# Block kernel on one core: the opening stage, its modulation products and its first norm, written anew

## The chip, the cores and the metric

The kernel runs on one core of one Trainium2 chip. The metric is the device time of one execution in microseconds (us); lower is better. In the tables of the profile PE is TensorE, PEld its weight loads, DVE is VectorE, ACT is ScalarE, POOL is GpSimd, and SP is SyncE, whose queue issues nearly all loads.

## The reference, cut to what matters

Two layers of a hybrid block are computed in fp32 for 256 tokens of x and 256 tokens of ctx, with a model width of 1024. Each layer first makes modulation vectors out of c and c_ctx, and then a half feed-forward block, a mixing block, and a second half feed-forward block. What the opening stage needs of it:

```python
mod_x = silu(c) @ ada_w + ada_b            # [9 * 1024]
mod_c = silu(c_ctx) @ ada_w + ada_b
sx, sc = split(mod_x, 9), split(mod_c, 9)  # shift, scale, gate, ...
h = x * rsqrt(mean(x * x) + EPS) * ffn1_norm
y = h * (1 + scale) + shift                # scale: chunk 1, shift: chunk 0
a, g = split(y @ wi, 2)                    # wi: 1024 x 5632
x = x + 0.5 * gate * ((silu(g) * a) @ wo)
```

The same is done for ctx with its own vectors. The first feed-forward block of layer 0 can begin only when shift (chunk 0) and scale (chunk 1) are there.

## The kernel before, in words

Features lie on partitions: x and ctx together are eight tiles of 128 features x 512 tokens (256 of x, 256 of ctx). A large product is made of three fp32r products of high and low parts (`mm3`, L181: lines 183, 184 and 185), so each weight tile is first split into a high part by ACT (L171) and a low part by DVE (L172).

The modulation weights come in slabs of 512 output columns and 1024 rows, 2 MB each, so that chunk 0 (shift) is slabs 0 and 1, and chunk 1 (scale) is slabs 2 and 3. `run` loads, in the order of the string `START = "02f1f3"`, slab 0, slab 2, the first up-weight tile (`f`, 1 MB), slab 1, the second up-weight tile and slab 3, behind the constants, the vectors and x. `ada_pe` makes the product of a slab: four rows (the high and the low part of c and of c_ctx) times the weights, one product for each of eight k tiles in plain fp32 (L301, for the first two k of slabs 0 and 1), or, for the others, two fp32r products (L298, L299) behind a split of the weight tile by ACT and DVE; then a copy of the row out of PSUM (L303), four small products that put the row on partitions (L306), and the bias (L308). `STARTC = "xr0s2d13D"` is the order in which this is written: sums of squares (x), the norm's factor (r), slab 0, the factor on all partitions (s: `spread`, L231 and L233), slab 2, the scale for features 0 to 511 (d: `derive`, L366), slabs 1 and 3, the scale for the other half (D).

`norm` (L427, L430, L431) multiplies x with scale and factor on DVE, adds the shift on ACT (which gives the high part yh), and makes the low part yl on DVE, tile by tile of 128 features x 256 tokens, the first four of the eight feature tiles first. `ffn` then runs the up-projections: 22 steps f, each 48 products of 128x512 (8 k tiles, value and gate, three products each), then SiLU (L550), the product with the value (L551) and the split of the result. In the first block the first two steps are woven: both take k 0 to 3, then both take k 4 to 7. Between the steps `fill` places pieces of other work (further modulation vectors on DVE, hyena filters).

A scheduler orders each engine's instructions by the order of the text and by when it reckons their inputs to be there; each engine then works strictly in that order. A product of plain fp32 is two instructions on PE, an fp32r product is one.

Of the kernel before, what the change touches and what calls it, by code (L numbers as in the profile page):

```python
# [9 lines left out]
F32 = mybir.dt.float32  # L10
# [29 lines left out]
LATE = (0, 0, 0, 0)  # L40
F1 = (1.9, 0, 1)
F2 = (0.8, 0, 1.0, 20)
WARM = 30
PIECES = 2
ADA = (6, 6, 8, 8)
START = "02f1f3"
STARTC = "xr0s2d13D"
# [13 lines left out]
class Builder:  # L61
    def __init__(self, ctx, tc, t, out):
        self.tc, self.nc, self.t, self.out = tc, tc.nc, t, out
        self.uid = 0
        self.ready = []
# [73 lines left out]
    def consts(self):  # L139
        nc, t = self.nc, self.t  # L140
        self.ident = self.const([P, P], name="ident")
        nc.sync.dma_start(out=self.ident, in_=t["k_ident"])
# [63 lines left out]
    def rsqrt_cols(self, ps, n):  # L206
        """ps [P, n, 2]: v and -v/2. One after the other column by column, so that the columns' chains overlap."""
# [17 lines left out]
    def bcast(self, r, ntile):  # L225
        """r [tokens, ntile] per token -> PSUM [128, ntile*128], the same on every partition."""
# [24 lines left out]
    def ada_init(self):  # L251
        nc, t = self.nc, self.t
        craw = self.const([P, KT, 2], name="craw")
        nc.sync.dma_start(out=craw, in_=t["cvec"])
        nc.scalar.activation(self.cvec, craw, AF.Silu)
        self.c4 = self.const([P, KT, 4], F32R, name="c4")
        for v in range(2):
            self.split(self.c4[:, :, 2 * v], self.c4[:, :, 2 * v + 1], self.cvec[:, :, v])
        self.c40 = self.const([P, KT, 4], name="c40")
        nc.gpsimd.memset(self.c40, 0.0)  # L260
        for v in range(2):
            nc.gpsimd.tensor_copy(self.c40[:, :, 2 * v], self.cvec[:, :, v])
        self.sum4 = self.const([4, 2], name="sum4")
        nc.gpsimd.dma_start(out=self.sum4, in_=t["k_sum4"])
# [9 lines left out]
    def ada_fetch(self, l, slab, pools):  # L274
        """The weights of a slab, by k."""
# [12 lines left out]
    def ada_pe(self, l, slab, ws, split):  # L288
# [3 lines left out]
        ps = self.pa((4, 512))  # L292
        for k, w in enumerate(ws):
            first, last = k == 0, k == KT - 1
# [7 lines left out]
        row = self.tmp((4, 512), name="row")  # L302
        nc.scalar.copy(row, ps)  # L303
# [7 lines left out]
    def ada_group(self, l, chunks, vecs):  # L311
        """Yields after each piece of work."""
# [72 lines left out]
    def sumsq(self, m, lo, n):  # L385
        """Adds the squares of tokens lo..lo+n of feature tile m."""
# [11 lines left out]
    def rstd(self, lo, n):  # L398
        """Each token's 1/rms, tokens on partitions."""
# [11 lines left out]
    def spread(self, lo, r):  # L411
        """The same on every partition."""
# [4 lines left out]
    def norm(self, l, name, T):  # L417
        nc = self.nc
        yh = [self.yp.tile([P, T], F32R, tag="y", name=self.nm("yh")) for _ in range(KT)]
        yl = [self.yp.tile([P, T], F32R, tag="y", name=self.nm("yl")) for _ in range(KT)]  # L420
        parts = 2 if self.ready else 1
        kp = KT // parts
        for v, ks in [(v, range(p * kp, p * kp + kp)) for p in range(parts) for v in range(T // S)]:
            s = slice(v * S, v * S + S)
            for k in ks:
                a = self.nyp.tile([P, S], F32, tag="ny", name=self.nm("ny"))
                nc.vector.scalar_tensor_tensor(a, self.x[k][:, s], self.gs[l, name, v][:, k:k + 1], self.rb[v],  # L427
                                               op0=ALU.mult, op1=ALU.mult)
                sh = self.shift(l, name, v)[:, k:k + 1]
                nc.scalar.activation(yh[k][:, s], a, AF.Identity, bias=sh)  # L430
                nc.vector.scalar_tensor_tensor(yl[k][:, s], a, sh, yh[k][:, s].bitcast(F32), op0=ALU.add, op1=ALU.subtract)  # L431
# [64 lines left out]
    def ffn(self, l, name, T, fill, last=1):  # L496
        nc = self.nc
        wi, wo = self.t[name + "_wi"][l], self.t[name + "_wo"][l]
        first = bool(self.ready)
        early = T == S and not first  # L500
        if early:
            zh, zl = self.scaled(l, name)
        yh, yl = self.norm(l, name, T)
        halves = [slice(v * S, v * S + S) for v in range(T // S)]

        def up(f, pieces=1):
            wh, wl = self.whl((P, 2 * KT, P))
            raw = self.ready.pop(0) if self.ready else self.load(wi[f])
            self.split(wh, wl, raw, pieces)
            return wh, wl, self.ps((P, T)), self.ps((P, T)), self.h((P, T), F32R, "hh"), self.h((P, T), F32R, "hl")  # L510
# [12 lines left out]
        def shifted(w):  # L523
            """What the norm's shift adds, per feature."""
            ps = self.pa((2, 2, P))
            wv = [a.rearrange("p (j k) n -> p k j n", j=2) for a in w[:2]]
# [12 lines left out]
        def late_act(w, c, rb):  # L539
            """act, for products that the norm's factor and shift are still to be applied to."""  # L540
# [7 lines left out]
        def act(w, s):  # L548
            sg = self.tmp((P, s.stop - s.start), name="sg")
            nc.scalar.activation(sg, w[2][:, s], AF.Silu)  # L550
# [915 lines left out]
```

## Time and profile before

| | |
|---|---|
| median of 3 runs | 1713.38 us (1712.46 to 1713.61) |
| the profiled execution's span | 1711.8 us, 1.6 us under the median |
| instructions | 23606 |
| PE busy | 1687.3 us (99%) |
| DVE, ACT busy | 1211.6 us (71%), 592.2 us (35%) |
| DMA | 262.56 MB, mean 153 GB/s |

The table counts work in the span of one profiled execution. The median is that of separate runs and holds what lies around the span too.

### The profile page before, as it was taken

What the parts mean: (1) busy time and instruction counts of PE and PEld (TensorE: products, weight loads), DVE (VectorE), ACT (ScalarE), POOL (GpSimd) and SP (SyncE); (2) the same over time, 40 slices, a digit from 0 to 9 for tenths busy, and PEclk for the clock granted to TensorE, in tenths of its full rate; (3) what the DMA queues carried; (4) which work ended last, traced back from release to release, by engine and by line L of the source; (5) the groups of instructions that cost most, each with busy time, mean ns of one, the idle gap of its engine ahead of it and who ended that gap; (6) DMA issues with size and microseconds to landing.
All of it is one profiled execution on the core that took longest, in us unless ns stands there. A gap on an engine that the chain in (4) does not pass through costs nothing.

```text
span 1711.8 us, 23606 instructions
## 1 busy us (share of the span) xinstructions
PE 1687.3 (99%) x9634; PEld 1441.0 (84%) x9634; DVE 1211.6 (71%) x2106; ACT 592.2 (35%) x766; POOL 34.1 (2%) x61
## 2 busy tenths in 40 slices
PE   8999999999999999999999999999999998999998
PEld 4788888878888898888888898888878897899998
DVE  6799965897675778888669876554464678875454
ACT  6432212333542433221222242221233254554343
POOL 0000000010000000000000000000000000000010
PEclk9999999999999999999999999999999999999999
DMA  9355543542232234545445425444432234344552
GB/s 371 128 200 194 186 172 146 175 164 99 81 112 99 78 141 161 184 164 195 151 147 202 174 77 194 172 160 160 150 124 99 93 129 161 108 159 175 181 195 75
DMA packets 50477, 262.56 MB, mean 153 GB/s; under 512 B 5802, under 2 KB 10736, under 8 KB 27584
## 3 DMA queue, kind: packets, MB, share of 16 engines
q1 hardware_dynamic: 48960, 257.05, 42.3%
q0 software_dynamic: 1408, 4.00, 0.6%
q8 instruction: 75, 1.23, 0.3%
q14 instruction: 34, 0.28, 0.0%
HBM read 257.88 MB, written 3.15 MB: 152 GB/s over the span
## 4 chain that ended last, share of the span: by engine, by line
PE 92%; DVE 3%; ACT 1%; issue 1%; DMA 0%; POOL 0%; DVEq 0%; ACTq 0%; POOLq 0%; SPq 0%
PE psm L183 29%; PE psm L184 28%; PE psm L185 28%; DVE acc L331 1%; ACT whi L171 1%; DVE wlo L172 1%; PE psa L989 1%; PE psa L1048 0%; PE psa L1226 0%; PE psa L1208 0%; PE psa L346 0%; PE psa L1028 0%; PE psa L891 0%; PE psa L1018 0%; PE psa L924 0%
## 5 line engine op out<-in xcount | busy, mean ns | idle before, releaser
L185 PE MATMUL psm<-yh,wlo 128*128 128x512 f32 (+1 forms) x1616 | 570.8, 354 | 1.4 <-DVE wlo L172 1.4
L184 PE MATMUL psm<-yl,whi 128*128 128x512 f32 (+1 forms) x1616 | 571.9, 355 | 0.1
L183 PE MATMUL psm<-yh,whi 128*128 128x512 f32 (+1 forms) x1616 | 570.3, 356 | 1.4 <-DVE glu L786 0.9
L171 ACT CAST whi<-raw 128x2048 fp32r<-128x2048 f32 (+3 forms) x171 | 303.9, 1779 | 598.8 <-PE psm L184 532.2
L172 DVE TENSOR_TENSOR wlo<-raw,whi 128x2048 fp32r<-128x2048 f32 (+3 forms) x171 | 363.8, 2128 | 134.4 <-ACT whi L171 134.0
L183 PEld LDWEIGHTS psm<-yh,whi 128*128 128x128 f32 x1616 | 305.1, 190 | 46.8 <-issue 2.3
L185 PEld LDWEIGHTS psm<-yh,wlo 128*128 128x128 f32 x1616 | 305.9, 189 | 44.8 <-DVE wlo L172 2.0
L184 PEld LDWEIGHTS psm<-yl,whi 128*128 128x128 f32 x1616 | 306.2, 190 | 43.0 <-DVE yl L431 0.8
L331 DVE SCALAR_TENSOR_TENSOR acc<-adaw,cvec,acc 128x512 f32<-128x512 f32 x392 | 274.7, 747 | 2.8
L183 PE MATMUL psm<-hh,whi 128*128 128x512 f32 (+1 forms) x752 | 265.1, 353 | 0.0
L185 PE MATMUL psm<-hh,wlo 128*128 128x512 f32 (+1 forms) x752 | 264.3, 352 | 0.0
L184 PE MATMUL psm<-hl,whi 128*128 128x512 f32 (+1 forms) x752 | 264.3, 351 | 0.0
L185 PEld LDWEIGHTS psm<-hh,wlo 128*128 128x128 f32 x752 | 142.3, 189 | 19.4 <-DVE acc L331 0.8
L184 PEld LDWEIGHTS psm<-hl,whi 128*128 128x128 f32 x752 | 142.3, 189 | 19.2 <-DVE hl L172 0.4
L183 PEld LDWEIGHTS psm<-hh,whi 128*128 128x128 f32 x752 | 142.2, 189 | 18.9 <-issue 0.2
L551 DVE TENSOR_TENSOR sg<-psm,sg 128x512 f32<-128x512 f32 (+1 forms) x90 | 54.4, 606 | 130.2 <-PE psm L185 120.2
L487 DVE SCALAR_TENSOR_TENSOR x<-psm,gt,x 128x256 f32<-128x256 f32 x112 | 50.5, 479 | 115.4 <-PE psm L185 115.3
L550 ACT ACTIVATE sg<-psm 128x512 f32<-128x512 f32 (+1 forms) x90 | 48.0, 533 | 211.6 <-PE psm L185 211.6
L389 ACT ACTIVATE sq<-x 128x512 f32<-128x512 f32 (+1 forms) x64 | 33.1, 522 | 90.4 <-DVE x L487 74.4
L183 PE MATMUL psm<-whi,yh 128*128 128x256 f32 (+1 forms) x200 | 58.2, 295 | 0.6 <-ACT whi L171 0.6
L184 PE MATMUL psm<-wlo,yh 128*128 128x256 f32 (+1 forms) x200 | 58.1, 293 | 0.0
L185 PE MATMUL psm<-whi,yl 128*128 128x256 f32 (+1 forms) x200 | 58.0, 293 | 0.0
(293 smaller groups left out, 1534.6 us busy)
## 6 DMA issues: line engine op xcount, KB each, us to landing
raw<-in_ffn_wi_dram SPq DMA_DIRECT2D x88, 1024.0 KB, 4.8
adaw<-in_ada_w_dram SPq DMA_DIRECT2D x68, 1024.0 KB, 5.0
raw<-in_ffn_wo_dram SPq DMA_DIRECT2D x32, 896.0 KB, 4.4
raw<-in_ffn_wo_dram SPq DMA_DIRECT2D x16, 1024.0 KB, 5.0
raw<-in_w_in_dram SPq DMA_DIRECT2D x14, 1024.0 KB, 4.7
raw<-in_w_out_dram SPq DMA_DIRECT2D x8, 1024.0 KB, 4.9
adaw<-in_ada_w_dram SPq DMA_DIRECT2D x16, 256.0 KB, 7.2
pm<-in_k_pool_dram SPq DMA_DIRECT2D x12, 256.0 KB, 2.8
```

The lines of the kernel that those rows point to most:

```text
L171: self.nc.scalar.copy(hi[:, s], src[:, s])
L172: self.nc.vector.tensor_tensor(lo[:, s], src[:, s], hi[:, s].bitcast(F32), op=ALU.subtract)
L183: mm(ps, lhsT=ah, rhs=bh, start=first, stop=False)
L184: mm(ps, lhsT=ah, rhs=bl, start=False, stop=False)
L185: mm(ps, lhsT=al, rhs=bh, start=False, stop=last)
L331: nc.vector.scalar_tensor_tensor(acc, ws[half][:, k, :], sc, acc, op0=ALU.mult, op1=ALU.add)
L389: nc.scalar.activation(sq, self.x[m][:, lo:lo + n], AF.Square)
L487: nc.vector.scalar_tensor_tensor(self.x[m][:, s], ps[:, v * S - lo:v * S - lo + S], gate[v][:, m:m + 1], self.x[m][:, s], op0=ALU.mult, op ...
L550: nc.scalar.activation(sg, w[2][:, s], AF.Silu)
L551: nc.vector.tensor_tensor(sg, w[3][:, s], sg, op=ALU.mult)
L989: nc.tensor.matmul(ps[par], lhsT=fwd[:, 2 * i + par, :], rhs=cur[par], start=True, stop=True)
```

## The change

The opening stage is a function of its own, `start`, written out by hand.

- **Products.** The weights of a slab are no longer split. `gemv` multiplies them in plain fp32 with 32 columns (c, c_ctx and 30 columns of zeros), k tile by k tile, and puts k on PSUM partitions 32 * (k % 4) and up: four column groups of TensorE. `ada_row` copies all 128 partitions out, and the four small products of `ada_end` add the groups up with a constant of 128 rows.
- **Order of loads.** c, x, slab 2, the vectors, two constants, slab 0, slab 3, the first up-weight tile, slab 1, the second up-weight tile.
- **Norm in two steps.** `norm_scale` and `norm_shift` are called apart, for k 0 to 3 and for k 4 to 7. PE, DVE and ACT take the stage in the order of the text (`manual_schedule`). The products of the first up-projection at k = 0 and k = 1 stand around the second half of slab 1's product; the two up-projections run one after the other.
- **Smaller edits.** 38 instead of 30 warm-up products; up-weights laid out k by k (index 2 * k + j instead of j * KT + k) in all feed-forward blocks, so that half a tile holds all the weights of half of the k; constants and c loaded in other places.

```diff
-WARM = 30
+WARM = 38
...
+        self.c32 = self.h((P, KT, 32), name="c32")
+        nc.gpsimd.memset(self.c32, 0.0)
+        nc.gpsimd.tensor_copy(self.c32[:, :, 0:2], self.cvec)
...
-            if k >= KT - split:
-                wh, wl = self.tmp((P, 512), F32R, "ah"), self.tmp((P, 512), F32R, "al")
-                self.split(wh, wl, w)
-                nc.tensor.matmul(ps, lhsT=self.c4[:, k, :], rhs=wh, start=first, stop=False)
-                nc.tensor.matmul(ps, lhsT=self.c4[:, k, :], rhs=wl, start=False, stop=last)
-            else:
-                nc.tensor.matmul(ps, lhsT=self.c40[:, k, :], rhs=w, start=first, stop=last)
...
+        for k in ks:
+            g = slice(32 * (k % 4), 32 * (k % 4) + 32)
+            self.nc.tensor.matmul(ps[g, :], lhsT=self.c32[:, k, :], rhs=ws[k], start=k < 4, stop=k >= KT - 4)
+
+    def ada_row(self, ps):
+        row = self.tmp((P, 512), name="row")
+        self.nc.scalar.copy(row, ps)
+        return row
...
-                self.mm3(w[2 + j][:, s], w[0][:, j * KT + k, :], w[1][:, j * KT + k, :], yh[k][:, s], yl[k][:, s], k == 0, k == KT - 1)
+                self.mm3(w[2 + j][:, s], w[0][:, 2 * k + j, :], w[1][:, 2 * k + j, :], yh[k][:, s], yl[k][:, s], k == 0, k == KT - 1)
...
+    def start(self):
...
+        craw = self.const([P, KT, 2], name="craw")
+        nc.sync.dma_start(out=craw, in_=self.t["cvec"])
+        self.load_x()
+        wi = self.t["ffn1_wi"][0]
+        ws = {2: self.ada_fetch(0, 2, (self.rawp, self.bigp))}
+        self.vectors()
+        self.sum4 = self.const([P, 2], name="sum4")
+        nc.sync.dma_start(out=self.sum4, in_=self.t["k_sum4"])
+        nc.sync.dma_start(out=self.ident, in_=self.t["k_ident"])
+        for slab in (0, 3):
+            ws[slab] = self.ada_fetch(0, slab, self.hp)
+        raws = [self.load(wi[0])]
+        ws[1] = self.ada_fetch(0, 1, self.hp)
+        raws.append(self.load(wi[1]))
...
+        with self.tc.manual_schedule(engines={et.PE, et.DVE, et.Activation}):
+            self.ada_init(craw)
+            self.warm_up()
+            for m in range(KT):
+                self.sumsq(m, 0, 512)
+            r = self.rstd(0, 512)
...
+            self.gemv(ws[2], every, acc[0])
+            self.spread(0, r)
+            self.ada_end(0, 2, self.ada_row(acc[0]))
+            self.derive(0, [1], two, 0, 4)
+            scale(first)
+            self.gemv(ws[0], every, acc[1])
+            self.ada_end(0, 0, self.ada_row(acc[1]))
+            shift(first)
+            acc = [self.ps() for _ in range(2)]
+            self.gemv(ws[3], every, acc[0])
+            row = self.ada_row(acc[0])
+            self.gemv(ws[1], first, acc[1])
+            self.ada_end(0, 3, row)
+            self.derive(0, [1], two, 4, 8)
+            split(0, 0)
+            scale(last)
+            split(0, 1)
+            mm(0, [0])
+            self.gemv(ws[1], last, acc[1])
+            row = self.ada_row(acc[1])
+            mm(0, [1])
+            self.ada_end(0, 1, row)
+            shift(last)
+            split(1, 0)
+            mm(0, range(2, KT))
+            self.act(up[0], slice(0, 512))
+            split(1, 1)
+            mm(1, every)
+            self.act(up[1], slice(0, 512))
...
-        self.ffn(0, "ffn1", 512, fill)
+        ys, ws = self.start()
+        self.ffn(0, "ffn1", 512, fill, 1, ys, ws)
```

Here `first` is k 0 to 3, `last` k 4 to 7 and `every` all eight; `split(i, p)` splits half p of up-weight tile i (ACT, then DVE), `mm(i, ks)` makes six products for each k of up-projection i, and `scale` and `shift` call the two steps of the norm for x and ctx.

## Rows read from the trace of the kernel before

**Rows 1.** The page: head, busy times with shares, chain that ended last by engine
```profile
span 1711.8 us, 23606 instructions
...
PE 1687.3 (99%) x9634; PEld 1441.0 (84%) x9634; DVE 1211.6 (71%) x2106; ACT 592.2 (35%) x766; POOL 34.1 (2%) x61
...
PE 92%; DVE 3%; ACT 1%; issue 1%; DMA 0%; POOL 0%; DVEq 0%; ACTq 0%; POOLq 0%; SPq 0%
```

**Rows 2.** Stretches: length; busy us (count) of five engines, granted clock, DMA share, GB/s
```profile
30.00:35.00 5.00, 4.83 (x14) 1.49 (x15) 3.91 (x8) 1.77 (x4) 0.00 (x0) 0.66 1.03 386
...
40.00:45.00 5.00, 5.00 (x19) 3.31 (x20) 4.96 (x11) 4.05 (x8) 0.00 (x0) 0.66 1.01 419
...
80.00:200.00 120.00, 120.00 (x535) 99.48 (x534) 111.02 (x174) 33.47 (x33) 1.07 (x2) 1.00 0.54 191
...
340.00:380.00 40.00, 39.56 (x178) 31.84 (x177) 39.64 (x66) 15.39 (x19) 6.74 (x8) 1.00 0.48 165
```

**Rows 3.** Timeline, first products, last of a slab, first-block SiLU: start, us, engine, line
```profile
41.21 1.31 PE L183 MATMUL psm<-yh,whi 128*128 128x512 f32 x3
...
51.21 0.39 PE L299 MATMUL psa<-al,c 128*4 128x512 f32 x1
...
68.98 0.60 ACT L550 ACTIVATE sg<-psm 128x512 f32<-128x512 f32 x1 [2.24 <-PE psm L185]
```

**Rows 4.** Groups of 0 to 69 us: busy, mean ns | idle before, releasers
```profile
L172 DVE TENSOR_TENSOR al<-adaw,ah 128x512 fp32r<-128x512 f32 x28 | 18.3, 687 | 1.8 <-issue 1.4 <-ACT ah L171 0.3
...
L430 ACT ACTIVATE yh<-ny,mods 128x256 fp32r<-128x256 f32 x16 | 7.7, 504 | 4.6 <-DVE ny L427 4.5
L431 DVE SCALAR_TENSOR_TENSOR yl<-ny,mods,yh 128x256 fp32r<-128x256 f32 x16 | 7.3, 479 | 0.2 <-ACT yh L430 0.2
...
L306 PE MATMUL psa<-sum,row 4*128 4x2 f32 x32 | 4.2, 249 | 2.5 <-ACT row L303 2.5
...
L172 DVE TENSOR_TENSOR wlo<-raw,whi 128x1024 fp32r<-128x1024 f32 x2 | 2.4, 1218 | 0.0
...
L303 ACT COPY row<-psa 4x512 f32<-4x512 f32 x4 | 2.3, 574 | 3.9 <-PE psa L299 3.9
...
L308 DVE TENSOR_TENSOR mods<-psa,vec 128x4 f32<-128x4 f32 x8 | 0.9, 156 | 3.7 <-PE psa L306 3.7
```

**Rows 5.** Timeline, SP's queue
```profile
0.73 0.40 SPq L142 DMA_DIRECT2D ident<-in_k_ident_dram  x1
...
2.15 3.76 SPq L383 DMA_DIRECT2D x<-in_xt_dram  x8
```

**Rows 6.** Tile x in 0 to 14 us: its eight loads, issue to landing
```profile
DMA to landing us min/median/max: 3.8/4.7/4.9
```

**Rows 7.** Timeline, ACT behind the two halves of slab 0
```profile
13.17 1.14 ACT L171 CAST ah<-adaw 128x512 fp32r<-128x512 f32 x2 [1.92 <-DMA adaw<-in_ada_w_dram]
...
15.68 0.62 ACT L171 CAST ah<-adaw 128x512 fp32r<-128x512 f32 x1 [1.38 <-DMA adaw<-in_ada_w_dram]
```

**Rows 8.** Timeline, PE: the warm-up products, and two plain fp32 products
```profile
0.98 8.43 PE L157 MATMUL psa<-ones 128*128 128x128 f32 x60 [0.98 <-POOL ones L144]
...
31.14 3.37 PE L301 MATMUL psa<-adaw,c 128*4 128x512 f32 x4
```

**Rows 9.** The chain in order of time: start, us, eight instructions of plain fp32
```profile
494.20 3.44 PE psa L989 x8
```

**Rows 10.** Timeline, PE: column groups of 64 (L1208) and of 32 (L1149)
```profile
503.18 1.04 PE L1208 MATMUL psa<-qbd,ke 128*64 128x256 f32 x8
504.15 0.32 PE L1149 MATMUL psa<-v,kdt 64*32 64x64 f32 x8
504.39 0.38 PE L183 MATMUL psm<-whi,yh 128*128 128x256 f32 x1
```

**Rows 11.** Timeline, PE: two of the up-projections' products, 30 products apart
```profile
80.12 0.39 PE L185 MATMUL psm<-yh,wlo 128*128 128x512 f32 x1
...
86.92 0.39 PE L185 MATMUL psm<-yh,wlo 128*128 128x512 f32 x1
```

More of the change, by code (lines that the diff above doesn't have):

```diff
@@ L286, in ada_fetch, with gemv, ada_end @@
         return ws
-    def ada_pe(self, l, slab, ws, split):
-        nc = self.nc
-        ps = self.pa((4, 512))
-        for k, w in enumerate(ws):
-            first, last = k == 0, k == KT - 1
-            if k >= KT - split:
-                wh, wl = self.tmp((P, 512), F32R, "ah"), self.tmp((P, 512), F32R, "al")
-                self.split(wh, wl, w)
-                nc.tensor.matmul(ps, lhsT=self.c4[:, k, :], rhs=wh, start=first, stop=False)
-                nc.tensor.matmul(ps, lhsT=self.c4[:, k, :], rhs=wl, start=False, stop=last)
-            else:
-                nc.tensor.matmul(ps, lhsT=self.c40[:, k, :], rhs=w, start=first, stop=last)
-        row = self.tmp((4, 512), name="row")
-        nc.scalar.copy(row, ps)
+    def gemv(self, ws, ks, ps):
+        for k in ks:
[5 more added lines that the diff above has]
+        return row
+    def ada_end(self, l, slab, row):
+        nc = self.nc
         pt = self.pa((P, 4, 2))
@@ L494, in part, with up_tiles, act, ffn @@
                     self.spread(lo, r)
[L496 removed]
+    def up_tiles(self, T):
+        wh, wl = self.whl((P, 2 * KT, P))
+        return wh, wl, self.ps((P, T)), self.ps((P, T)), self.h((P, T), F32R, "hh"), self.h((P, T), F32R, "hl")
+    def act(self, w, s):
+        nc = self.nc
+        sg = self.tmp((P, s.stop - s.start), name="sg")
+        nc.scalar.activation(sg, w[2][:, s], AF.Silu)
+        nc.vector.tensor_tensor(sg, w[3][:, s], sg, op=ALU.mult)
+        self.split(w[4][:, s], w[5][:, s], sg)
+    def ffn(self, l, name, T, fill, last=1, ys=None, done=()):
         nc = self.nc
         wi, wo = self.t[name + "_wi"][l], self.t[name + "_wo"][l]
[L499 to L500 removed]
+        early = T == S
         if early:
             zh, zl = self.scaled(l, name)
[L503 removed]
+        yh, yl = ys or self.norm(l, name, T)
+        act = self.act
         halves = [slice(v * S, v * S + S) for v in range(T // S)]
         def up(f, pieces=1):
[L507 to L510, printed above, removed]
+            w = self.up_tiles(T)
+            self.split(w[0], w[1], self.load(wi[f]), pieces)
+            return w
         def mm(w, k, s):
             for j in range(2):
[L514 removed]
+                self.mm3(w[2 + j][:, s], w[0][:, 2 * k + j, :], w[1][:, 2 * k + j, :], yh[k][:, s], yl[k][:, s], k == 0, k == KT - 1)
         def shift_parts():
@@ L568, in ffn @@
                         late_act(w, c, rb)
-                for p in range(2 if first else 0):
-                    for w in ws:
-                        for k in range(4 * p, 4 * p + 4):
-                            mm(w, k, slice(0, T))
-                        if p == 1:
-                            act(w, slice(0, T))
-                for v, s in enumerate(halves if not (first or early) else []):
+                for s in halves if not (done or early) else []:
                     for w in ws:
@@ L1255, in finish, with scale, shift, mm @@
             nc.sync.dma_start(out=self.out[j, :, h * 512:h * 512 + 512], in_=o)
+    def start(self):
+        nc = self.nc
+        craw = self.const([P, KT, 2], name="craw")
[12 more added lines that the diff above has]
+        raws.append(self.load(wi[1]))
+        nc.sync.dma_start(out=self.tneg, in_=self.t["k_tneg"])
+        et = mybir.EngineType
+        two = [0, 1]
+        with self.tc.manual_schedule(engines={et.PE, et.DVE, et.Activation}):
[4 more added lines that the diff above has]
+            r = self.rstd(0, 512)
+            yh = [self.yp.tile([P, 512], F32R, tag="y", name=self.nm("yh")) for _ in range(KT)]
+            yl = [self.yp.tile([P, 512], F32R, tag="y", name=self.nm("yl")) for _ in range(KT)]
+            up = [self.up_tiles(512) for _ in range(2)]
+            half = slice(0, KT), slice(KT, 2 * KT)
+            every, first, last = range(KT), range(4), range(4, KT)
+            ny = {}
+            def scale(ks):
+                for k in ks:
+                    ny[k] = self.tmp(name="ny")
+                    for v in two:
+                        self.norm_scale(0, "ffn1", k, v, ny[k][:, v * S:v * S + S])
+            def shift(ks):
+                for k in ks:
+                    for v in two:
+                        self.norm_shift(0, "ffn1", k, v, ny[k][:, v * S:v * S + S], yh, yl)
+            def mm(i, ks):
+                w = up[i]
+                for k in ks:
+                    for j in range(2):
+                        self.mm3(w[2 + j], w[0][:, 2 * k + j, :], w[1][:, 2 * k + j, :], yh[k], yl[k], k == 0, k == KT - 1)
+            def split(i, p):
+                self.split(up[i][0][:, half[p]], up[i][1][:, half[p]], raws[i][:, half[p]])
+            acc = [self.pa() for _ in range(2)]
+            self.gemv(ws[2], every, acc[0])
[27 more added lines that the diff above has]
+            self.act(up[1], slice(0, 512))
+        return (yh, yl), up
@@ L1257, in run @@
     def run(self):
         self.spec = [self.drp.tile([2, 2, P, 512], F32, tag=f"spec{l}", name=f"spec{l}") for l in range(2)]
-        self.vectors()
-        self.ada_init()
-        self.warm_up()
-        self.load_x()
-        nc = self.nc
-        nc.sync.dma_start(out=self.tneg, in_=self.t["k_tneg"])
-        raw, big = self.rawp, self.bigp
-        ws = {}
-        for step in START:
-            if step == "f":
-                self.ready.append(self.load(self.t["ffn1_wi"][0, len(self.ready)]))
-            else:
-                ws[int(step)] = self.ada_fetch(0, int(step), (raw, big) if len(ws) < 2 else self.hp)
@@ L1336, in _constants @@
     k["k_sel"] = sel.reshape(P, 4 * P)
-    k["k_sum4"] = np.array([[1, 0], [1, 0], [0, 1], [0, 1]], f)
+    k["k_sum4"] = np.array([[p % 32 == v for v in range(2)] for p in range(P)], f)
     blk = np.zeros((P, 2), f)
```

75 lines of the change are left out of this document (22 added, 53 removed).

## The prediction, made before the changed kernel was seen

> **What bounds the kernel now.** I read the page first: PE is busy for 99% of a span of 1711.8 us, and the chain that ended last is 92% PE [rows 1]. So nearly everywhere a microsecond counts only if PE spends or waits it. The stretches then show where the opening stands apart: from 80 to 200 us PE is busy without a gap at the full clock, while from 30 to 45 us the granted clock averages 0.66 in two of the stretches shown, and the loads run flat out, at 386 to 419 GB/s [rows 2].
>
> The timeline gives the marks. The first product of an up-projection starts at 41.21 us, the last product of a slab at 51.21, and the SiLU of the second up-projection, which waits for its last product, at 68.98 [rows 3]. From there PE goes on with the third up-projection, which the change leaves as it is. So the question is one number: when is the second up-projection's last product out? Before, that is 69.0 us.
>
> What held it back is in the groups: 28 low parts of modulation weights cost DVE 18.3 us, with their 28 high parts on ACT ahead of them [rows 4], though the slabs land much faster: ACT waits for the two halves of slab 0 at 13.17 and 15.68 us, so one MB lands in 2.51 us [rows 7].
>
> **The change part by part.**
>
> *Loads.* Before, the eight tiles of x are issued from 2.15 to about 5.5 us, behind three small loads that cost 0.47 us each (0.73 to 2.15) [rows 5]; the last lands up to 4.9 us after its issue [rows 6], at 10.4. Two of the three now come later, so x is in at 9.5. Ahead of the first half of slab 1 lie slabs 2, 0 and 3, one up-weight tile, that half itself (8 MB) and 0.2 MB of vectors and constants. At 2.51 us per MB that is 20.6 us: landed at 30.1. I take 30.5, for the vectors come in small pieces; this half us is an estimate. Its second half lands at 33.
>
> *What falls away.* All 28 splits, 18.3 us of DVE and their part of ACT [rows 4]. That makes DVE and ACT wait for loads and products, no longer the other way.
>
> *What is on the path from 30.5 us.* PE takes its work in the written order:
> - The product of k = 3 of slab 1 can only follow its load. Two plain fp32 products took 3.37 us where the clock averaged 0.66 [rows 8, 2], 1.69 each; eight instructions took 3.44 us elsewhere [rows 9], 0.86 a product. PE has little to do between slabs, so I take the lower level (1.2 GHz): 32.2.
> - Four small products for slab 3: 4.2 / 4 = 1.05 us [rows 4]. They stand behind slab 1's half though slab 3 landed 5 us earlier. Then bias and scale, four small DVE operations like L308's of 0.156 us: 0.5 together. 33.7.
> - DVE makes the low half of the first up-weight tile only after these: 1.22 us [rows 4], 34.9. Until then PE stops at the third product of k = 0.
> - Four products of k = 0. An up-product costs (86.92 - 80.12) / 30 = 0.227 us at full clock [rows 11], twice that at the lower: 1.8, so 36.7.
> - The second half of slab 1: four products, one per column group. If the groups work side by side, this is one product's 1.7 us: 38.4.
> - Six products of k = 1, 1.4 us at full clock, 2.7 at half; I take 2.0, the clock rising meanwhile: 40.4. They cover the copy of the row, 0.57 us on ACT [rows 4]; without them that copy would be idle time.
> - Four small products, 1.05: 41.4.
> - 84 further products, 84 x 0.227 = 19.0 us: 60.4.
>
> *What I cost at nothing.* The second step of the norm for k 4 to 7 follows at 41.6: eight operations of about 0.5 us on ACT and on DVE [rows 4]. The first pair of tiles is out near 43; the 12 products of k = 2 and 3 cover PE until 44.1, and each further k gives PE 1.36 us for 1.0 us of DVE. Uncovered, it would cost some 2 us. The second tile's low halves (1.22 each) fall behind these steps and behind the first SiLU; PE has 8 and 5 us of products ahead of each. The first half of the norm ends near 28, while DVE would only wait. Eight more warm-up products are 16 instructions of 0.14 [rows 8], 2.2 us at most, run while slab 2 is still landing. The other weight layout changes no size and no count of any load or product; the further blocks wait for hardly anything (PE is busy for 99%), so I give it 0, and at most 0.5 either way.
>
> *Do column groups work side by side?* The trace has no product with four groups, 128 rows and 512 columns, so I bound it. Eight instructions on two groups of 64 with 256 columns took 1.04 us [rows 10]; one after another they would take half of the 3.44 us that eight of 512 columns take [rows 9], 1.72. Eight on four groups of 32 with 64 columns took 0.32 [rows 10], against 0.43 and the last one's tail by the same measure. The groups did overlap. One end of the price of a half slab is then one product's time (0.86 or 1.7), the middle twice that, the other end four times; I take the first, since the nearest row (groups of 32) is nearest to it.
>
> The Trainium skill speaks against such changes of form: "TensorEngine Tiling (Array Packing)", Key Properties, says that switching the tiling mode drains TensorE. In the row, the ordinary product that follows the eight on groups of 32 starts at 504.39, before their 0.32 us are over at 504.47 [rows 10]; no longer drain shows. By the rule at its worst, a whole 0.32 us at each of three switches on the path, the sum would be 61.4 in place of 60.4.
>
> **Sum.** 69.0 - 60.4 = 8.6 us earlier. Everything after it is bound by PE and ordered relative to it, so it moves as a whole: 1711.8 - 8.6 = 1703.2 us of span, and with the 1.6 us by which the median of the runs lies above the profiled span, **1704.8 us** (-0.5%).
>
> *Both ends.* With the full clock throughout, the tail, the ten products of k = 0 and 1 and the half slab cost 0.84 + 0.9 + 0.6 + 0.84 = 3.2 us less: 57.2, a gain of 11.8, 1701.6 us. With the loads 2 us late, only two groups side by side at the lower level (+1.7) and that level held for eight more up-products (+1.8), 65.9: a gain of 3.1, 1710.3.
>
> **The rivals.**
> 1. *The change's main device does not work: groups one after another, at full clock.* Then 32 products of 0.86 stand on PE: from 13.7 (warm-up to 11.6, sums of the norm about 2), 27.5 for products, 9.3 for what stands between them (spreading 1.1, small products 4 x 1.05, 0.5 and 1.2 on DVE, ten up-products 2.3) and 19.0: 69.5, **1713.9 us**, no change. Against it: both rows of groups.
> 2. *The other sign: groups one after another, at the lower clock.* The place is the same; at 1.69 us, the only price the opening itself shows [rows 8], 32 products take 54.1: 96.1, 27 us later, **1740 us**. It decides from 0.84 us a product, where the sum reaches 69.0, and from 0.95 the kernel is slower by over 0.2%. The rows of groups speak against it as well.
> 3. *Given back later.* From 340 to 380 us DVE is busy for 39.64 of 40 us and PE shows its first idle time [rows 2]. If DVE does not come earlier by as much as PE, PE waits there; with half lost, **1709 us**. Against it: DVE's filling work starts behind the up-projections and is ordered by them, and DVE was idle for less before.
>
> **Chances.** The forecast's mechanism, its ends included, 0.85; rival 1 0.05, rival 2 0.03, rival 3 0.07. 0.2% (3.4 us) is about what a measurement of this kernel can tell from no change. Faster by more: 0.87; within it: 0.08 (rival 1, some of rival 3 and of the slow end); slower: 0.05 (rival 2, and a little for an order that the scheduler lays worse). The range runs from a little under the full-clock end to shortly before the slow end: 1701.0 to 1709.5.
>
> **What would show it.** Right: no low parts of modulation weights on DVE; the instructions of `gemv` starting in packs of four; first product of an up-projection near 32 to 35 us; DVE waiting for small products and ACT or PE for loads; the second SiLU near 60.5; PE without a gap from there to 340, each later mark earlier by the same 8 to 9 us. Wrong: slab products at 0.43 us per instruction one behind another; PE idle between 41 and 60 us, waiting for yl or for a low half; slabs landing later than 2.51 us per MB; a new gap of PE between 340 and 380.

## The result and the profile after

The changed kernel takes **1703.97 us** (median of four runs, 1703.79 to 1705.70) against 1712.92 us for the kernel before beside it (1711.58 to 1713.61): a ratio of 0.9948, 95% interval 0.9934 to 0.9962. The forecast was 1704.8, in a range of 1701.0 to 1709.5. The profiled span went from 1711.8 us [rows 1] to 1702.1, 9.7 us less. Unchanged and run again later beside nine runs of the kernel before, it gave 1703.76 us and a ratio of 0.9944 (0.9932 to 0.9957).

The page of the changed kernel: head, busy times with shares, the chain that ended last.

```profile
span 1702.1 us, 23539 instructions
...
PE 1678.8 (99%) x9650; PEld 1440.4 (85%) x9650; DVE 1193.8 (70%) x2077; ACT 575.8 (34%) x737; POOL 33.6 (2%) x59
...
PE 92%; DVE 3%; DMA 2%; ACT 1%; issue 1%; SPq 0%; POOL 0%; DVEq 0%; ACTq 0%; POOLq 0%
```

The kernel as a whole looks as it did in [rows 1]: TensorE still sets the end. DMA has gone from 0% to 2% of the chain, because the opening is now paced by its loads. The timeline of PE in the opening (start, us, line) shows this.

```profile
30.41 3.08 PE L280 MATMUL psm<-adaw,c 128*32 128x512 f32 x8 [2.14 <-DMA adaw<-in_ada_w_dram]
33.42 1.05 PE L291 MATMUL psa<-sum,row 128*128 128x2 f32 x8
34.33 0.48 PE L177 MATMUL psm<-yh,whi 128*128 128x512 f32 x1
...
36.13 0.50 PE L179 MATMUL psm<-yh,wlo 128*128 128x512 f32 x1 [1.09 <-DVE wlo L166]
...
37.26 1.06 PE L280 MATMUL psm<-adaw,c 128*32 128x512 f32 x8
38.25 0.50 PE L177 MATMUL psm<-yh,whi 128*128 128x512 f32 x1
...
40.56 0.49 PE L177 MATMUL psm<-yh,whi 128*128 128x512 f32 x1
```

The first product of an up-projection comes at 34.33 instead of 41.21 [rows 3]. Its third product waits 1.09 us for wlo, as forecast. The eight instructions of the second half of slab 1 (four products) take 1.06 us in all: on the four column groups they cost little more than one product. The next fences are the timeline of PEld at four landings (the second half of slab 2, the last k of slab 0, and the last two k of slab 1's first half), that of ACT at the second SiLU, and some stretches (columns as in [rows 2]).

```profile
14.36 0.16 PEld L280 LDWEIGHTS psa<-adaw,c 128*32 128x32 f32 x8 [0.98 <-DMA adaw<-in_ada_w_dram]
...
21.84 0.18 PEld L280 LDWEIGHTS psa<-adaw,c 128*32 128x32 f32 x2 [0.49 <-DMA adaw<-in_ada_w_dram]
...
31.76 0.14 PEld L280 LDWEIGHTS psm<-adaw,c 128*32 128x32 f32 x2 [0.54 <-DMA adaw<-in_ada_w_dram]
32.44 0.14 PEld L280 LDWEIGHTS psm<-adaw,c 128*32 128x32 f32 x2 [0.55 <-DMA adaw<-in_ada_w_dram]
```

```profile
59.69 0.60 ACT L495 ACTIVATE sg<-psm 128x512 f32<-128x512 f32 x1 [7.39 <-PE psm L179]
```

```profile
30.00:35.00 5.00, 4.59 (x18) 1.74 (x18) 0.49 (x5) 1.70 (x2) 0.00 (x0) 1.00 1.06 409
35.00:40.00 5.00, 3.91 (x23) 2.32 (x22) 5.00 (x10) 0.59 (x1) 0.00 (x0) 1.00 1.02 415
40.00:45.00 5.00, 5.00 (x26) 4.21 (x26) 3.86 (x11) 4.07 (x9) 0.00 (x0) 1.00 1.01 415
...
330.00:370.00 40.00, 39.26 (x177) 31.47 (x176) 39.64 (x66) 15.39 (x19) 6.73 (x8) 1.00 0.49 164
...
410.00:420.00 10.00, 9.10 (x58) 8.48 (x57) 9.56 (x34) 5.01 (x9) 1.19 (x3) 0.83 0.37 126
```

The second SiLU is at 59.69 instead of 68.98 [rows 3], 9.29 us earlier, and the end is 9.7 earlier: nothing of it is given back (the further 0.4 us is not traced). The stretch where VectorE is full, now ten us earlier on the clock, holds 39.26 us of PE and 39.64 of DVE, against 39.56 and 39.64 [rows 2]. One thing differs from what was expected: the granted clock of the opening is 1.00 (2.4 GHz) from 30 to 45 us, where it was 0.66 in two of three such stretches before.

### The profile page after: what moved, and what is told of

Its sections match the earlier page's. It is cut to its first block, busy times and chain, and to the rows that moved or that the text cites. A ratio compares the mean times of both kernels' runs of the same rounds, so it can differ in the third digit from the quotient of the medians.

```text
span 1702.1 us, 23539 instructions
## 1 busy us (share of the span) xinstructions
PE 1678.8 (99%) x9650; PEld 1440.4 (85%) x9650; DVE 1193.8 (70%) x2077; ACT 575.8 (34%) x737; POOL 33.6 (2%) x59
## 4 chain that ended last, share of the span: by engine, by line
PE 92%; DVE 3%; DMA 2%; ACT 1%; issue 1%; SPq 0%; POOL 0%; DVEq 0%; ACTq 0%; POOLq 0%
PE psm L177 29%; PE psm L178 28%; PE psm L179 28%; DVE acc L316 1%; ACT whi L165 1%; DVE wlo L166 1%; DMA adaw<-in_ada_w_dram 1%; DMA pm<-in_k_pool_dram 1%; PE psa L979 1%; DMA vec<-in_vecs_dram 1%; PE psa L1216 0%; PE psa L1038 0%; PE psa L1198 0%; PE psa L331 0%; PE psa L881 0%
```

## The experiments

All times stand beside runs of the kernel before on the same chip; its medians there are 1713.43 (first four experiments), 1714.73 (next four), 1714.16 (next three) and 1713.67 us (last). "Second SiLU" is the mark of [rows 3] in the profiled execution.

| kernel | median us | ratio to before, 95% | second SiLU, us |
|---|---|---|---|
| one_group | 1714.96 | 1.0003 (0.9993 to 1.0012) | 72.45 |
| before_groups | 1712.25 | 0.9987 (0.9978 to 0.9997) | 69.42 |
| before_order | 1716.96 | 1.0018 (1.0008 to 1.0027) | 75.54 |
| no_weave | 1705.73 | 0.9952 (0.9937 to 0.9967) | 63.16 |
| vec_first | 1705.21 | 0.9948 (0.9933 to 0.9963) | 61.28 |
| big_rows | 1703.94 | 0.9945 (0.9929 to 0.9962) | 60.46 |
| early_small | 1701.14 | 0.9926 (0.9911 to 0.9941) | 57.87 |
| woven | 1701.33 | 0.9926 (0.9912 to 0.9941) | 57.34 |
| after_again | 1703.76 | 0.9944 (0.9932 to 0.9957) | 62.14 |
| early_fill | 1701.40 | 0.9935 (0.9921 to 0.9948) | 58.24 |
| woven_fill | 1701.81 | 0.9927 (0.9915 to 0.9940) | 57.16 |
| woven_fill12 | 1698.56 | 0.9915 (0.9902 to 0.9929) | 55.93 |

**One column group.** All k go to the same 32 columns, and the copy and the small products take these 32 rows; all else is as changed.

```diff
-            g = slice(32 * (k % 4), 32 * (k % 4) + 32)
-            self.nc.tensor.matmul(ps[g, :], lhsT=self.c32[:, k, :], rhs=ws[k], start=k < 4, stop=k >= KT - 4)
+            self.nc.tensor.matmul(ps[:32, :], lhsT=self.c32[:, k, :], rhs=ws[k], start=k == 0, stop=k == KT - 1)
...
```

> The changed kernel, but all eight k tiles of a slab go to the same 32 PSUM partitions, one column group, so that nothing can run side by side; the sums come out the same. Theory (the products are cheap only because four column groups run side by side): a product costs 0.86 us in sequence, slab 1's second half and the slabs before it pile up on TensorE, the second SiLU moves from 59.7 to about 69 us and the time to about 1713, the gain gone. Rival (the loads are the bound and the products hide behind them anyway): at most 2 us more than the changed kernel, 1704 to 1706.

The timeline of PE in one_group:

```profile
32.99 10.49 PE L279 MATMUL psm<-adaw,c 128*32 128x512 f32 x24
...
44.39 0.50 PE L177 MATMUL psm<-yh,whi 128*128 128x512 f32 x1
```

One behind another, an instruction costs 10.49 / 24 = 0.44 us, a product 0.87. The first up-product comes 10 us later than in the changed kernel, and the whole gain is gone: rival 1, near its price (1713.9 us and a second SiLU at 69.5 forecast; 1714.96 and 72.45 measured).

**Column groups alone.** The kernel before, with its own loads and its planner's order, but `gemv`'s products in place of the splits.

```diff
-            if k >= KT - split:
-                wh, wl = self.tmp((P, 512), F32R, "ah"), self.tmp((P, 512), F32R, "al")
-                self.split(wh, wl, w)
...
+            g = slice(32 * (k % 4), 32 * (k % 4) + 32)
+            nc.tensor.matmul(ps[g, :], lhsT=self.c32[:, k, :], rhs=w, start=k < 4, stop=k >= KT - 4)
```

> The kernel before with one part of the change alone: the modulation products in plain fp32 on four column groups, no splits; load order, norm and the scheduler's order as before. Theory (the 28 splits on VectorE and ScalarE held the opening up): most of the gain comes from this alone; the second SiLU comes at 57 to 61 us in place of 69.0, the time 1702 to 1706. Rival (the order of loads and the stage written out by hand bring the gain): the second SiLU stays above 66 us, 1710 to 1714.

A miss: the second SiLU came at 69.42, and the rival's numbers held. The timeline of PE in before_groups:

```profile
34.00 0.73 PE L183 MATMUL psm<-yh,whi 128*128 128x512 f32 x2 [4.32 <-ACT yh L420]
...
41.76 1.05 PE L291 MATMUL psa<-adaw,c 128*32 128x512 f32 x4
...
43.86 1.05 PE L291 MATMUL psa<-adaw,c 128*32 128x512 f32 x2
```

The planner's order puts two up-products ahead of the last product of slab 1 (34.66 us), and TensorE waits 4.32 us for yh there. It then scatters slab 3's products, one or two at a time, among the up-products: two instructions alone take as long (1.05 us) as eight in a pack (1.06 above). In six such pieces, from 41.76 to 51.57 us, the eight products cost 6.3 us where two packs would take 2.1, and the groups pay in full only where four products stand together. These 4.2 us are not the whole difference of 9.7 us to the changed kernel's second SiLU; the pauses for yh are part of the rest. The ten runs spread from 1707.71 to 1713.65 us, and their median is no gain beyond 0.2%. Four of them lie at 1707.71 to 1709.78; the profile is of one of the other six and does not show what was better in those four.

**Order of slabs alone.** The kernel before, with the slabs loaded and used in the changed kernel's order.

```diff
-START = "02f1f3"
-STARTC = "xr0s2d13D"
+START = "203f1f"
+STARTC = "xr2s0d31D"
```

> The kernel before with another part alone: slabs loaded and used in the order of the changed kernel (2, 0, 3, first up-weight tile, 1, second up-weight tile), the products still split. Theory: the 28 splits still cost VectorE 18 us and stay on the path, so 1711 to 1715, no gain. Rival (the order brings it): 1704 to 1708.

The timeline of PE, and a stretch, in before_order:

```profile
44.78 0.59 PE L299 MATMUL psa<-al,c 128*4 128x512 f32 x1 [1.41 <-DVE al L172]
...
58.92 0.39 PE L299 MATMUL psa<-al,c 128*4 128x512 f32 x1
```

```profile
45.00:50.00 5.00, 5.00 (x16) 3.29 (x14) 1.91 (x5) 2.01 (x4) 0.00 (x0) 0.53 0.57 210
```

With the splits still there, TensorE waits until 44.78 us for a low part of slab 3, the up-products behind start at a granted clock of 0.53, and the last product of slab 1, the last slab, comes at 58.92 (51.21 before [rows 3]). The order alone gains nothing, as expected; it costs 0.18%, and 1716.96 us lies above the 1711 to 1715 expected.

**No products between the norm's steps.** As changed, but all products of the first up-projection follow the second half of slab 1.

```diff
-            mm(0, [0])
             self.gemv(ws[1], last, acc[1])
             row = self.ada_row(acc[1])
-            mm(0, [1])
...
-            mm(0, range(2, KT))
+            mm(0, every)
```

> The changed kernel with one part undone: no product of the first up-projection stands between the norm's two steps; all of its 48 products follow the last small products of slab 1. Theory (until 36.1 us TensorE can do no up-product but two anyway, and slab 1's second half is in by 35.2): its first product comes at about 38 us, the 96 products end at 59 to 60 us, and the time stays within 1 us of the changed kernel, 1703 to 1705. Rival (the weave is worth its 12 products): 2.7 us more, 1706 to 1707.

The timeline of PE and a stretch of no_weave:

```profile
37.23 1.36 PE L291 MATMUL psa<-sum,row 128*128 128x2 f32 x8 [0.84 <-ACT row L284]
...
39.03 0.63 PE L178 MATMUL psm<-yl,whi 128*128 128x512 f32 x1
39.46 0.63 PE L179 MATMUL psm<-yh,wlo 128*128 128x512 f32 x1
```

```profile
40.00:45.00 5.00, 5.00 (x14) 3.89 (x13) 4.49 (x12) 3.62 (x9) 0.00 (x0) 0.53 1.01 413
```

The second SiLU is 3.5 us later, but not for idle time: TensorE waits 0.84 us for the row here, and 1.09 for wlo in the changed kernel. The difference is the clock: some 15 up-products run 0.43 us apart instead of 0.23, 3.0 us, and slab 1's first half takes 3.95 instead of 3.08. By time it is 1.8 us slower than the changed kernel, between the expectation (within 1) and the rival (2.7), and the two intervals overlap. Whether the order brought this clock was open, so the changed kernel was profiled again.

**The changed kernel once more**, with no edit.

> The changed kernel once more, unaltered, as the mark for the two runs beside it on the same chip. My theory (its profile has a stretch at 410 to 420 us where the granted clock is 0.83, and the profiles of three of its variants have none, so the stretch belongs to the execution and not to the kernel): the second SiLU again at 59.7 us, the step of some 1.6 us near 414 may be missing, the median within 1.5 us of 1704.0. Rival (the stretch belongs to the kernel's order): it is there again at the same place.

The timelines of PE, PEld and ACT, and stretches, of after_again:

```profile
30.72 3.75 PE L280 MATMUL psm<-adaw,c 128*32 128x512 f32 x8 [2.14 <-DMA adaw<-in_ada_w_dram]
34.39 1.05 PE L291 MATMUL psa<-sum,row 128*128 128x2 f32 x8
...
38.77 1.94 PE L280 MATMUL psm<-adaw,c 128*32 128x512 f32 x8
...
43.06 0.47 PE L177 MATMUL psm<-yh,whi 128*128 128x512 f32 x1
```

```profile
32.75 0.18 PEld L280 LDWEIGHTS psm<-adaw,c 128*32 128x32 f32 x2 [0.50 <-DMA adaw<-in_ada_w_dram]
```

```profile
62.14 0.60 ACT L495 ACTIVATE sg<-psm 128x512 f32<-128x512 f32 x1 [7.34 <-PE psm L179]
```

```profile
30.00:35.00 5.00, 4.28 (x14) 1.33 (x14) 0.00 (x0) 1.99 (x2) 0.00 (x0) 0.66 1.05 400
35.00:40.00 5.00, 3.91 (x19) 1.65 (x18) 4.51 (x13) 0.00 (x0) 0.00 (x0) 0.75 1.02 418
...
410.00:420.00 10.00, 9.10 (x71) 8.48 (x71) 9.43 (x35) 4.75 (x9) 1.19 (x3) 1.00 0.19 48
```

The same kernel, but the clock is low from 30 to 40 us, and the second SiLU is 2.45 us later. The stretch at 410 us with a granted clock of 0.83 is missing, which accounts for up to 1.7 us of why the ends lie only 0.5 us apart. Half of the expectation failed (59.7 us again), half held (the stretch at 410 belongs to the execution). So no_weave shows 1.0 us against this execution and 3.5 against the other: what the weave itself is worth stays open.

**Two edits of the loads.** vec_first issues the vectors ahead of x; big_rows loads slabs 0 and 3 as halves of 1 MB.

```diff
+        self.vectors()
         self.load_x()
...
-        self.vectors()
```

> The changed kernel with the vectors' load issued ahead of x instead of between slabs 2 and 0. My theory (the vectors' short rows take about 2 us of the queue between slab 2 and slab 0, where 1 was forecast, and every later slab lands that much later): slab 1's first half lands near 31 us instead of 32.44, the first up-product near 34.7 instead of 36.13, the time 1 to 2 us under the changed kernel's. Rival (the vectors cost as much ahead of x, since everything behind them is late by the same): landings and time unchanged within 0.7 us.

```diff
-        for slab in (0, 3):
-            ws[slab] = self.ada_fetch(0, slab, self.hp)
...
+            for half in range(2):
+                w = pool.tile([P, 4, 512], F32, tag=tag, name=self.nm("adaw"))
+                nc.sync.dma_start(out=w, in_=self.t["ada_w"][0, slab][:, half * 4:half * 4 + 4])
...
```

> The changed kernel with slabs 0 and 3 loaded as 1 MB halves in rows of 8 KB, instead of 256 KB pieces in rows of 2 KB. My theory (pieces land at 0.68 us per 256 KB, 2.7 us per MB, and the wide rows of the up-projection's weights at 2.51): two slabs of 2 MB land 0.8 us earlier in all, slab 1's first half near 31.7 us, the time about 0.7 us under the changed kernel's. Rival (the pace is the memory's, not that of the rows): landing within 0.3 us of 32.44.

Timelines of PEld, vec_first and then big_rows, at the last k of slab 1's first half, and a stretch of big_rows:

```profile
32.51 0.14 PEld L280 LDWEIGHTS psm<-adaw,c 128*32 128x32 f32 x2 [0.54 <-DMA adaw<-in_ada_w_dram]
```

```profile
31.67 0.14 PEld L280 LDWEIGHTS psm<-adaw,c 128*32 128x32 f32 x2 [0.54 <-DMA adaw<-in_ada_w_dram]
```

```profile
35.00:40.00 5.00, 4.60 (x16) 2.20 (x17) 4.61 (x10) 0.59 (x1) 0.00 (x0) 0.66 1.02 420
```

Where the vectors stand in the queue is no matter (32.51 against 32.44): my theory missed and the rival held, they cost the same ahead of x. The wide rows bring the landing 0.77 us earlier, as my theory had it. But this execution's clock was 0.66 from 35 to 40 us, its second SiLU is 0.77 us later than in the changed kernel's first profile, and the time is the same, where 0.7 us less was expected.

**Small products first.** As changed, with one line moved and slab 1's product in one piece.

```diff
             row = self.ada_row(acc[0])
-            self.gemv(ws[1], first, acc[1])
             self.ada_end(0, 3, row)
...
             mm(0, [0])
-            self.gemv(ws[1], last, acc[1])
+            self.gemv(ws[1], every, acc[1])
```

> The changed kernel with one step moved: slab 3's eight small products go ahead of slab 1's packed products, which then run in one piece after the first up-product. My theory (what sets the first up-product is the chain slab 1's first half landed at 32.44 us, its product, the small products of slab 3 at 33.42, the norm's vectors on VectorE, wlo at 34.86, product at 36.13): the small products now wait for slab 3's row alone, start near 29 to 30 us, the first up-product near 32.5, the second SiLU near 57.5, and the time is about 2 us under the changed kernel's. Rival (slab 1's end, not the first product, sets the second SiLU): second SiLU stays within 0.5 us of 59.7 and the time within 0.7 us of the changed kernel's.

The timeline of PE in early_small:

```profile
28.81 1.05 PE L291 MATMUL psa<-sum,row 128*128 128x2 f32 x8 [0.73 <-ACT row L284]
...
31.91 0.59 PE L179 MATMUL psm<-yh,wlo 128*128 128x512 f32 x1 [0.52 <-DVE wlo L166]
...
33.71 2.83 PE L280 MATMUL psm<-adaw,c 128*32 128x512 f32 x16
```

My theory held: the small products no longer stand behind a load, the third product comes 4.2 us earlier, the second SiLU at 57.87 and the time 2.8 us below the changed kernel's. The intervals of the two ratios overlap, but each of its four runs (1700.38 to 1701.94 us) lies below all nine of the changed kernel (1702.89 and up), though the kernel before was no faster beside it. This is the step "they stand behind slab 1's half though slab 3 landed 5 us earlier" of the prediction, shown to be on the path.

**Up-products between the slabs.** The up-weights are loaded ahead of slabs 3 and 1, and the products of k 0 to 3 stand ahead of slab 3's (first up-projection) and around slab 1's (second). `end` is `ada_end`, with `derive` behind it for slab 3.

```diff
+        ws[0] = self.ada_fetch(0, 0, self.hp)
+        raws = [self.load(wi[i]) for i in range(2)]
+        for slab in (3, 1):
...
+            mm(0, first)
+            self.gemv(ws[3], every, acc)
+            row = self.ada_row(acc)
+            mm(1, [0])
+            end(3, row)
+            scale(last)
+            mm(1, [1])
...
+            self.gemv(ws[1], every, acc)
...
```

> The changed kernel with another order of the opening: the loads run slab 2, vectors, slab 0, both up-projections' first weights, slab 3, slab 1, and products of both up-projections that need only the first half of the norm stand between and ahead of the packed products of slabs 3 and 1. My theory (TensorE has no work from about 27 to 36 us other than what lands late, and up-products whose rows are ready can fill it): first up-product near 27 us, second SiLU near 54.5, the time about 5 us under the changed kernel's. Rival (what VectorE and ScalarE must do ahead of the products, two casts and two remainders more and the norm's first half, comes too late for them): first product past 31 us, second SiLU within 1 us of 59.7.

The timeline of PE, and a stretch, in woven:

```profile
26.39 0.50 PE L177 MATMUL psm<-yh,whi 128*128 128x512 f32 x1 [1.56 <-ACT yh L423]
27.63 0.50 PE L178 MATMUL psm<-yl,whi 128*128 128x512 f32 x1 [0.74 <-DVE yl L424]
...
31.62 0.39 PE L179 MATMUL psm<-yh,wlo 128*128 128x512 f32 x1
```

```profile
25.00:30.00 5.00, 2.87 (x7) 2.07 (x8) 4.54 (x12) 5.00 (x11) 0.00 (x0) 0.81 1.04 383
```

The first product came when expected, the second SiLU 2.8 us late. After the pauses of 1.56 and 0.74 us, the next products run some 0.43 us apart, from 27.97 up to 31.62 us: nine of them lose 3.65 - 9 x 0.227 = 1.6 us, and the wait for yl costs 0.74 more.

**Constant matmuls in the pause.** If the pause costs the clock, work that means nothing should give it back. early_fill adds 14 to early_small, woven_fill 20 to woven, each ahead of the first up-product.

```diff
+            def fill(n):
+                ps = self.pa((P, P))
+                for i in range(n):
+                    nc.tensor.matmul(ps, lhsT=self.ones, rhs=self.ones, start=True, stop=True)
...
+            fill(14)
             mm(0, [0])
```

> early_small with 14 matmuls of a constant (128 columns each, result not used) ahead of the first up-product, where TensorE had nothing to do between 29.86 and 31.9 us. My theory (the lower granted clock of 0.72 in 30 to 35 us follows the pauses just before, and the products of slab 1 and the three up-products ahead of it ran at 2.83 and 0.43 us for that reason): the granted clock stays near 1.00 in 30:35, slab 1's sixteen products take about 1.9 to 2.1 us, the second SiLU comes at about 56.8, the time about 1 us under early_small's 1701.1. Rival (the clock falls whatever stands there, or the added matmuls only delay the chain): second SiLU at 57.9 or later.

> woven with 20 matmuls of a constant ahead of the first up-product, between 24.8 and 27.6 us, where TensorE waited for the norm's first rows (its first product came at 26.39, the second at 27.63, and the next nine ran 0.43 us apart at a granted clock of 0.81 to 0.85). My theory (the pause ahead of them cost the clock, and this cost 9 x 0.2 = 1.8 us): the up-products run 0.23 us apart from the first on, the second SiLU comes at about 55.6 instead of 57.34, the time about 1.7 us under woven's 1701.3. Rival (the products were slow for another reason, or the fillers hold TensorE up): second SiLU at 57.3 or later.

The timeline of PE and a stretch in early_fill, then the timeline of PE in woven_fill:

```profile
30.29 3.37 PE L1305 MATMUL psa<-ones 128*128 128x128 f32 x28
33.42 0.48 PE L177 MATMUL psm<-yh,whi 128*128 128x512 f32 x1
...
34.99 1.92 PE L280 MATMUL psm<-adaw,c 128*32 128x512 f32 x16
```

```profile
30.00:35.00 5.00, 5.00 (x40) 4.46 (x41) 4.25 (x12) 2.00 (x2) 0.00 (x0) 1.00 1.06 408
```

```profile
24.44 4.71 PE L1304 MATMUL psa<-ones 128*128 128x128 f32 x40
28.91 0.48 PE L177 MATMUL psm<-yh,whi 128*128 128x512 f32 x1
```

The clock was as my theory had it: 1.00 in every stretch from 25 to 45 us in both, slab 1's sixteen instructions in early_fill 1.92 us instead of 2.83, products 0.23 us apart. But a plain fp32 matmul is two instructions, so the filling took twice what I had reckoned, and what the clock gave back it took away: the second SiLU missed both expectations (58.24 and 57.16 us), and neither time gained. So the last run has fewer.

```diff
-            fill(20)
+            fill(12)
```

> woven_fill with 12 matmuls of the constant instead of 20. In woven_fill the 20 ran as 40 instructions of 0.12 us and took 4.71 us, from 24.44 to 28.9, so that the first up-product came at 28.91 and its second part at 29.23, where the rows that they need were there by 27.63. My theory (the constant matmuls keep the granted clock at 1.00, and those beyond 27.3 us only delay): 24 instructions end at about 27.3, the second part of the first product comes at about 27.7, the nine products behind it stay 0.23 us apart, the second SiLU comes near 55.7, and the time is 1 to 1.5 us under woven_fill's 1701.8. Rival (the clock of the opening differs from one execution to the next whatever TensorE did before): products 0.43 us apart for some stretch between 28 and 45 us, and the second SiLU at 57 or later.

The timeline of PE, and a stretch, in woven_fill12:

```profile
24.89 2.92 PE L1304 MATMUL psa<-ones 128*128 128x128 f32 x24
...
27.89 0.43 PE L178 MATMUL psm<-yl,whi 128*128 128x512 f32 x1
```

```profile
25.00:30.00 5.00, 5.00 (x35) 4.53 (x35) 4.48 (x11) 5.00 (x11) 0.00 (x0) 1.00 1.05 387
```

The marks came as my theory expected: products 0.23 us apart from 27.9, second SiLU at 55.93. The time, 1698.56 us, fell by 3.2 us against woven_fill where 1 to 1.5 was expected; the second SiLU accounts for 1.2 of it. That mark is 13.1 us below the one of [rows 3], and the ratio of 0.9915 (0.9902 to 0.9929) lies clear of after_again's 0.9944 (0.9932 to 0.9957): woven and its filling together are faster than the changed kernel, and this is the lowest median of this study. The filling's own part is not shown by time: the intervals of woven (0.9912 to 0.9941) and woven_fill12 overlap, and what shows it is one profile of each, 57.34 against 55.93 us. The granted clock of whole executions points the same way here (0.995 to 0.996 in the four runs of woven, 0.996 to 0.998 in the five of woven_fill12), but not for early_small (0.997 to 0.998) and early_fill (0.993 to 0.997).

## Why the prediction was right, step by step

The forecast of the time was 0.8 us off, the second SiLU 0.7 (60.4 forecast, 59.69 measured). Two terms were mis-sized, by +1.9 and -2.8 us, and in the first profile they nearly cancel: that the mark came within 0.7 us is luck, for the clock of an execution was not foreseen. after_again has the clock where I had put it, and its second SiLU is 1.7 us late; its time agrees even so, mostly because the low stretch near 410 us, which the kernel before had too, is missing there. The mechanism (packs on four column groups, an opening paced by its loads) came as forecast.

| step | forecast end | first profile | after_again |
|---|---|---|---|
| slab 1's first half landed | 30.5 | 32.44 | 32.75 |
| its last product | 32.2 | 33.42 | 34.39 |
| small products, bias and scale, wlo | 34.9 | 36.13 | 37.11 |
| four products of k = 0 | 36.7 | 37.26 | 38.77 |
| second half of slab 1 | 38.4 | 38.25 | 40.63 |
| six products of k = 1 | 40.4 | 39.75 | 42.26 |
| four small products | 41.4 | 40.56 | 43.06 |
| 84 products | 60.4 | 59.69 | 62.14 |

- **Landing, too early by 1.9 to 2.3 us.** The step that failed is "at 2.51 us per MB ... I take 30.5"; one of the prediction's signs of being wrong, slabs landing later than 2.51 us per MB, came true. The four last landings of that half in the first profile lie 0.68 us apart (31.76 and 32.44 above), so slabs that come in pieces of 256 KB take 2.7 us per MB; the 2.51 of [rows 7] was read from halves of 1 MB. On the 5 MB that come in pieces (slabs 0 and 3, half of slab 1) this is 1.0 us, and big_rows gives 0.77 us of it back on two slabs. The rest lies between slabs 2 and 0. Slab 2 was in at 14.36 us, 0.2 before its place in the sum, and slab 0 at 21.84. Its eight pieces of 0.68 us take 5.4 us of that, the vectors and constants 2.0, where the sum had 0.9 for them (0.2 MB at 2.51 us and the estimated 0.4). vec_first shows that the place of the vectors does not matter.
- **The clock, too low in one profile and right in the other.** Between "its last product" and "four small products" the sum has 41.4 - 30.5 = 10.9 us. At a granted clock of 1.00 it took 8.1 (32.44 to 40.56), with 0.66 and 0.75 from 30 to 40 us it took 10.3 (32.75 to 43.06). The full-clock end of the prediction covered the first; the other is the sum as forecast with the landing late.
- **Column groups side by side: right.** One half slab costs one product's time: 1.06 us for eight instructions at full clock, 1.94 at the lower level, against 0.44 each, one behind another, in one_group. By the Trainium skill ("TensorEngine Tiling (Array Packing)", Key Properties), changing the tiling mode drains TensorE. Here the next ordinary product starts at 38.25, before the pack's 1.06 us from 37.26 are over: as in [rows 10], no drain of 0.32 us shows. What could be one is small: the product ahead of the pack starts 0.32 us before it, and the first one behind it 0.34 us before the next, where 0.23 is usual; but the first product behind the small products, at 40.56, also takes 0.32.
- **The rivals.** Rivals 1 and 2 are out, and one_group shows that rival 1's price was nearly right (3 us too low at the second SiLU, 1.1 at the end). Rival 3 is out: 9.29 us at the second SiLU, 9.7 at the end.
- **What I had not weighed.** I took the order and the groups as one mechanism. before_groups and before_order show that neither alone gains more than 0.2% here (0.9987 and 1.0018), and one_group that the rest of the change without the groups gains nothing (1.0003). That packs have to be kept together and slab 1 has to be fed last is my reading of these profiles; no run has the groups and the new order of loads under the planner, and none undoes the two-step norm, the layout of the up-weights or the extra warm-up products by themselves.

## What to carry to other kernels

Narrow products on separate column groups cost one product for four only if the four stand next to each other in the instruction stream; here a planner that scattered a slab's eight products spent 6.3 us on them where two packs take 2.1. A product that waits for a load should not stand ahead of small work that is ready and that others wait for: moving one line, with slab 1's product joined into one piece, was worth 2.8 us. Where a stretch is latency-bound, compare the granted clock of the profiles before reading a difference of 2 or 3 us as the edit's work, and try a few constant matmuls in the pause, no longer than the pause is: in the profiles the clock stayed up with them, though their gain in time is not clear of the noise here.

## What the runs showed of the hardware

- The granted clock in the opening differs between executions of one kernel: the second SiLU came at 59.69 and at 62.14 us. The Trainium skill ("TensorE: Matmul & The Clock Gate", Part 1) says that what runs at the lower clock varies from run to run of the same kernel; these two profiles agree. The three filled kernels show a granted clock of 1.00 in every stretch from 25 to 45 us, as does one_group, where PE is busy for 19.28 of these 20 us; of the kernels with more pauses only the changed kernel's first profile shows the same. These are single profiles.
- Two short stretches later in the run, with a granted clock of 0.83 over ten us (at most 1.7 us each), near 410 and 1360 us, come and go between executions: the first is in the profiles of the kernel before and of the changed kernel, and not in after_again; the second is in all of these and not in that of before_order. What brings them was not found.
- Loads in pieces of 256 KB (rows of 2 KB) landed 0.68 us apart, while halves of 1 MB (rows of 8 KB) took 2.51 us: 2.7 against 2.5 us per MB.
- On column groups of 32, two instructions alone take 1.05 us (before_groups), eight on four groups take 1.06 (the changed kernel), both at a granted clock of 1.00.
